# A two-layer hybrid mixer kernel: other start addresses of its buffers in SBUF, and another matmul cost in its planner

## The chip, the cores and the metric

The kernel runs on one core of one Trainium2 chip. The metric is the device time of one execution in microseconds (us), as the median of the runs shown. The core has five engines that run side by side: TensorE (PE, matrix multiplications; its weight loads are listed apart as PEld), VectorE (DVE), ScalarE (ACT), GpSimd (POOL) and SyncE (SP, which here only issues DMAs). Operands of the engines lie in SBUF, 128 partitions wide; a tile's address is its byte offset within each partition. Results of matmuls go to PSUM.

## What is computed

A sequence of 256 tokens of width 1024 goes through two layers in fp32. Each layer is a gated feed-forward block, a mixer with three branches (a gated linear recurrence, windowed attention, a gated delta rule), and another feed-forward block:

```
for l in range(2):
    x = x + 0.5 * swiglu(rms_norm(x, g1[l]), w_gate1[l], w_up1[l], w_down1[l])   # 1024 -> 2816 -> 1024
    u = rms_norm(x, gm[l])
    proj = u @ w_in[l]                                # 1024 -> 11536 columns
    ya, yb, yc = rg_lru(proj), attention(proj), delta_rule(proj)
    y = sum of sigmoid(gates) * (ya @ wa, yb @ wb, yc @ wc)
    x = x + y @ w_out[l]
    x = x + 0.5 * swiglu(rms_norm(x, g2[l]), w_gate2[l], w_up2[l], w_down2[l])
```

## The kernel before

**Tiling.** Activations are kept transposed, 128 channels on the partitions and the 256 tokens along the row: one such block is 128x256 fp32, 1024 bytes of each partition. Weights are read from HBM in blocks of up to 1024 columns into six buffers `raw0` to `raw5` (line 598 issues each DMA on SP's queue), and each block is split into two fp32r parts, `wh` (the rounded value, mostly by ACT) and `wl` (the rest, by DVE), in five buffers of each kind, 4096 bytes of a partition each. Activations are split in the same way. A product is then three fp32r matmuls that are added up in PSUM: high by high, low by high, high by low.

**The two forms of the main matmul.** In `stationary` (feed-forward and most of the mixer) a 128x128 piece of `wh` or `wl` is the stationary operand and a 256-column activation block is the moving one; a piece starts 512 bytes after the one before it. There are 11280 such matmuls. In `moving` (attention's queries, keys and values) the roles are swapped: 128 columns of an activation block are stationary, and 256 columns of `wh` or `wl` are moving. There are 864 of those. A first small product in each mixer uses pieces of only 64 columns. Beside these there are fp32 matmuls and transposes for the norms, the attention and the delta rule, whose operands lie mostly in one large tile, `arena`.

**Places in SBUF.** Tiles are placed one after the other, in the order in which `Prog.__init__` asks for them, each at a multiple of 32 bytes. `cst` begins at byte 16512. Before the change this gives `raw0` at 26560, `wh0` at 51136, `wl0` at 71616, `X` at 92096, then `zr`, `ssq`, `eps_n`, `half`, `tiny` at 102400, `arena` at 106496, and the 60 activation slots `s0` to `s59` (`Slots`, 1024 bytes each) from 163840. All sizes from `raw0` to `ssq` are multiples of 1024 bytes, and so are those of `tiny`, `arena` and the slots. So every `raw`, `wh`, `wl` buffer, `X`, `zr` and `ssq` begins 64 bytes below a multiple of 1024 (960 modulo 1024), and `tiny`, `arena` and all slots begin at one. Slots hold the split activations that the main matmuls read; a block of 256 columns that finds no slot free goes to `arena`, whose parts begin at multiples of 256 bytes.

**What sets the order.** The order of the instructions on each engine is fixed when the program is written out. `Prog` keeps a clock for each engine; each instruction that is written adds its estimated cost (`Engine._cost`) to its engine's clock. After every main matmul `pump` looks which side task (a conversion, a piece of the delta rule, a norm) is due by PE's clock, and writes its next step there. So PE's queue is one fixed sequence, the main matmuls with the side tasks' small matmuls between them, and the estimate for one main matmul decides after how many of them a side task's next step stands. The estimate for an fp32r matmul is

```
            if lhsT.dtype == F32R:
                return max(0.46 * n, 0.83 * m)
```

with n the moving and m the stationary columns: 0.46 x 256 = 117.8 ns.

Of the kernel before, what the change touches and what calls it, by code (L numbers as in the profile page):

```python
# [10 lines left out]
F32 = mybir.dt.float32  # L11
# [6 lines left out]
P = 128  # L18
# [21 lines left out]
KEEP, KEEP2 = 3072, 2048  # L40
ARENA_COLS = 14336
NSLOT = 60
SPARE = 4
SLACK = (800.0, 1500.0, 1500.0, 1500.0, 1500.0, 600.0)
URGENT = 2
# [54 lines left out]
def flat_chunks():  # L100
    return [c for layer in all_jobs() for jobs in layer for job in jobs for c in job[2]]


def group_chunks(chunks):
    groups, cur, cols = [], [], 0
    for c in chunks:
        w = c[3] * c[5]
        if cur and cols + w > GROUP_COLS:
            groups.append((cur, cols))
            cur, cols = [], 0  # L110
        cur.append(c)
        cols += w
    groups.append((cur, cols))
    return groups
# [60 lines left out]
class Arena:  # L175
    def __init__(self, pr, ap, unit):
        self.pr, self.ap, self.unit = pr, ap, unit
        self.n = ap.shape[1] // unit
        self.busy = [False] * self.n
        self.stamp = [0.0] * self.n  # L180
        self.peak = 0
# [123 lines left out]
def _free(ap):  # L305
    n = 1
    for x in ap.shape[1:]:
        n *= x
    return n


class Engine:
# [16 lines left out]
    def _cost(self, name, a, k):  # L329
        key = self._key  # L330
        if key == "pe":
            lhsT = k["lhsT"] if name == "matmul" else a[1]
            rhs = k["rhs"] if name == "matmul" else a[2]
            n, m = _free(rhs), _free(lhsT)
            if lhsT.dtype == F32R:
                return max(0.46 * n, 0.83 * m)
            if name == "transpose":
                return 0.84 * max(n, m)
            if m <= 32 and lhsT.shape[0] <= 32:
                return 40.0  # L340
            if m <= 64 and lhsT.shape[0] <= 64 and n <= 64:
                return 100.0
            return 1.7 * max(n, m)
        n = _free(a[0])
        if name == "tensor_reduce":
            n = _free(a[1])
        if key == "a":
            c = 93 + 0.833 * n
            for x in ("scale", "bias", "accum_out"):
                c += 93 * (not isinstance(k.get(x, 0.0), float) and x in k)  # L350
            func = a[2] if name == "activation" else None
            sets = TABLES.get(func)
            if sets and self._pr.table not in sets:
                self._pr.table = sets[0]
                c += 1283
            return c
        if key == "g":
            return (330 + 160 * n) if k.get("op") == ALU.pow else 350 + 0.6 * n
        if name == "reciprocal":
            return 68 + 6.3 * n  # L360
        fast = name in ("tensor_copy", "tensor_scalar") and a[1].space != PSUM
        c = 68 + (0.52 if fast else 1.04) * n
        if name in ("scalar_tensor_tensor", "tensor_scalar") and not isinstance(a[2], float):
            c += 60
        if k.get("accum_out") is not None:
            c += 60
        return c
# [5 lines left out]
class Prog:  # L373
    def __init__(self, ctx, tc, io):
        self.tc, self.nc, self.io = tc, tc.nc, io
        nc = self.nc
        self.clock = {"pe": 0.0, "v": 0.0, "a": 0.0, "g": 0.0}
        self.table = None
        self.cur = self.main = Task(None, 0.0, 0)
        self.step, self.used = set(), {}  # L380
        self.tasks = []
        self.pe, self.v = Engine(self, "pe", nc.tensor), Engine(self, "v", nc.vector)
        self.a, self.g = Engine(self, "a", nc.scalar), Engine(self, "g", nc.gpsimd)
        sb = ctx.enter_context(tc.tile_pool(name="sb", bufs=1))
        ps = ctx.enter_context(tc.tile_pool(name="ps", bufs=1, space=PSUM))
        dr = ctx.enter_context(tc.tile_pool(name="dr", bufs=1, space=bass.MemoryType.DRAM))
        self.cst = sb.tile([P, CST["_n"]], F32, name="cst")
        self.prm = sb.tile([P, L * PRM["_n"]], F32, name="prm")
        self.raw = [sb.tile([P, GROUP_COLS], F32, name=f"raw{i}") for i in range(NRAW)]
        self.wh = [sb.tile([P, 1024], F32R, name=f"wh{i}") for i in range(NCONV)]  # L390
        self.wl = [sb.tile([P, 1024], F32R, name=f"wl{i}") for i in range(NCONV)]
        self.X = sb.tile([P, KD, T], F32, name="X")
        self.zr = sb.tile([P, T], F32, name="zr")
        self.ssq = sb.tile([P, T], F32, name="ssq")
        self.eps_n = sb.tile([P, 1], F32, name="eps_n")
        self.half = sb.tile([P, 8], F32, name="half")
        self.tiny_t = sb.tile([P, 1024], F32, name="tiny")
        self.ar_t = sb.tile([P, ARENA_COLS], F32, name="arena")
        self.tiny = Arena(self, self.tiny_t, 8)
        self.slots = Slots(self, sb, NSLOT)  # L400
        self.ar = Arena(self, self.ar_t, 64)
        self.big = Banks(self, [ps.tile([P, 512], F32, name=f"big{i}") for i in range(NBIG)])
        self.sm = Banks(self, [ps.tile([P, 512], F32, name=f"sm{i}") for i in range(8 - NBIG)])
        self.gdram = [dr.tile([16, P], F32, name=f"gd{l}") for l in range(L)]
        self.rdram = [[dr.tile([P, 64], F32, name=f"rd{l}_{i}") for i in range(4)] for l in range(L)]
        self.rc = [self.tiny.get(16).ap for _ in range(L)]
        self.ea = [self.tiny.get(8) for _ in range(L)]
        self.qg = [self.tiny.get(6) for _ in range(L)]
        self.groups = group_chunks(flat_chunks())
        self.chunk_at = []  # L410
        off = 0
        self.goff = []
        for gi, (cs, cols) in enumerate(self.groups):
            self.goff.append(off)
            c0 = 0
            for c in cs:
                self.chunk_at.append((c, gi, c0, c[3] * c[5]))
                c0 += c[3] * c[5]
            off += P * cols
        self.unread = [len(cs) for cs, _ in self.groups]  # L420
        self.cursor = 0
        self.dma_next = 0
        self.dma_clock = 0.0
        self.raw_t = {}
        self.conv_t = {}
        self.conv_next = 0
        self.when = {}
        self.ops = {}
        self.prepared = set()
        self.nsq = None  # L430
        self.npair = 4
# [111 lines left out]
    def get(self, cols):  # L543
        b = None
        if cols == T:
            b = self.slots.get(F32, SPARE)
        return b or self.ar.get(cols, self.keep())
# [1157 lines left out]
```

## Time and profile before

| what | before |
|---|---|
| median of 3 runs | 1631.65 us (1627.21, 1631.65, 1632.0) |
| the profiled execution | 1627.63 us, of which the span from first to last instruction is 1625.4 us |
| granted TensorE clock, mean | 0.994 |
| PE busy | 1602.4 us (99%) |
| DVE, ACT, POOL busy | 71%, 58%, 9% |
| DMA | 279 MB, 172 GB/s, 54% of the 16 engines' time |

The stages in the profiled execution, by the first and last main matmul of each: layer 0 feed-forward 6 to 198 us, mixer 198 to 631, feed-forward 631 to 819; layer 1 feed-forward 819 to 1006, mixer 1006 to 1434, feed-forward 1434 to 1622. A record of a matmul is longer than the interval to the next one's start, since matmuls overlap in the array; the pace is read from starts. A row of the timeline merges instructions of one kind that follow each other, and one period of the main stream (three matmuls) takes two rows.

### The profile page before, as it was taken

To read this page: it belongs to the slowest core of one execution; us is meant where nothing else is said; L and a number is where in the kernel's file an instruction comes from. 1 tells how busy PE (TensorE), PEld (TensorE's weight loads), DVE (VectorE), ACT (ScalarE), POOL (GpSimd) and SP (SyncE) were. 2 spreads that over 40 slices of the span, in tenths; PEclk is the share of its full clock that TensorE was granted. 3 is DMA by queue.
4 is the path that set the end of the run, shared out by engine and by line. 5 is a ranking of instruction groups with operands and counts; after the bars stand their busy time and mean duration, and the time that the engine had idled before them with its cause. 6 is when DMAs were issued, how large, how long until landed. Compare 5 with 4: busy or idle time off the path is not lost. (4 is left out here: it accounts for less than half of the span.)

```text
span 1625.4 us, 34428 instructions
## 1 busy us (share of the span) xinstructions
PE 1602.4 (99%) x13952; PEld 1560.0 (96%) x13952; DVE 1159.2 (71%) x2172; ACT 936.7 (58%) x1643; POOL 139.3 (9%) x280
## 2 busy tenths in 40 slices
PE   9999999999999999999999999999999999999999
PEld 8999999989988999999999999999898899999999
DVE  8666588987973667666566656989878756676653
ACT  7544456878854546444454445568887555554442
POOL 0000000345002000000000000003540120000000
PEclk9999999999998999999999999999999999999999
DMA  8655656544343565555555555656443345655562
GB/s 304 186 187 179 193 179 194 164 162 133 120 129 107 163 204 184 187 188 178 188 192 183 182 185 185 195 176 182 139 140 122 123 131 189 190 184 185 181 188 86
DMA packets 84942, 279.04 MB, mean 172 GB/s; under 512 B 10256, under 2 KB 15664, under 8 KB 84784
## 3 DMA queue, kind: packets, MB, share of 16 engines
q1 hardware_dynamic: 84784, 276.85, 53.7%
q8 instruction: 109, 1.79, 0.4%
q14 instruction: 49, 0.40, 0.1%
HBM read 275.49 MB, written 1.33 MB: 170 GB/s over the span
## 5 line engine op out<-in xcount | busy, mean ns | idle before, releaser
L323 PE MATMUL big<-s,wh 128*128 128x256 f32 (+1 forms) x7520 | 1346.3, 281 | 7.0 <-DVE s L323 6.0
L323 PEld LDWEIGHTS big<-s,wh 128*128 128x128 f32 (+1 forms) x7520 | 1151.0, 188 | 17.4 <-DVE s L323 6.8
L323 PE MATMUL big<-s,wl 128*128 128x256 f32 (+1 forms) x3760 | 1053.6, 280 | 0.0
L323 DVE TENSOR_TENSOR wl<-raw,wh 128x1024 fp32r<-128x1024 f32 (+3 forms) x523 | 620.8, 1187 | 248.4 <-ACT wh L323 245.2
L323 ACT ACTIVATE wh<-raw 128x1024 fp32r<-128x1024 f32 (+4 forms) x497 | 509.1, 1025 | 361.8 <-PE big L323 168.8
L323 PEld LDWEIGHTS big<-s,wl 128*128 128x128 f32 (+1 forms) x3760 | 705.3, 188 | 2.8 <-issue 1.8
L323 ACT ACTIVATE s<-s 128x256 fp32r<-128x256 f32 (+1 forms) x213 | 85.2, 413 | 116.6 <-DVE s L323 116.0
L323 POOL TENSOR_TENSOR tiny<-tiny,half 128x4 f32<-128x4 f32 (+1 forms) x28 | 38.6, 1378 | 1102.0 <-DVE tiny L323 1083.9
L323 PE MATMUL sm<-arena 128*128 128x128 f32 (+7 forms) x1440 | 114.0, 238 | 9.7 <-DVE arena L323 6.9
L323 PEld LDWEIGHTS sm<-arena 32*32 32x32 f32 (+5 forms) x1440 | 85.8, 138 | 30.2 <-issue 9.3
L323 PE MATMUL big<-wh,s 128*128 128x256 f32 x576 | 110.2, 287 | 0.0
L323 POOL TENSOR_TENSOR arena<-arena 128x60 f32<-128x60 f32 (+14 forms) x240 | 98.6, 411 | 62.6 <-DMA arena<-rd 44.7
L323 DVE TENSOR_TENSOR s<-s,s 128x256 fp32r<-128x256 f32 (+1 forms) x181 | 75.7, 422 | 36.5 <-ACT s L323 36.1
L323 PEld LDWEIGHTS big<-wh,s 128*128 128x128 f32 x576 | 89.6, 189 | 1.2
L323 DVE SCALAR_TENSOR_TENSOR s<-big,prm,s 128x255 f32<-128x255 f32 (+2 forms) x183 | 85.6, 477 | 6.6 <-ACT s L323 5.3
L323 DVE TENSOR_TENSOR arena<-big,zr 128x512 f32<-128x512 f32 x88 | 60.9, 692 | 34.8 <-PE big L323 34.5
L323 PE MATMUL big<-wl,s 128*128 128x256 f32 x288 | 82.1, 285 | 0.0
L323 ACT ACT_TABLE_LOAD x63 | 80.8, 1283 | 1.7 <-PEq L1697 0.7
L323 ACT ACTIVATE arena<-sm 128x128 f32<-128x128 f32 (+6 forms) x152 | 48.8, 323 | 37.6 <-PE sm L323 35.1
L323 ACT ACTIVATE s<-big 128x256 f32<-128x256 f32 x53 | 20.2, 382 | 62.1 <-PE big L323 62.1
L323 PEld LDWEIGHTS big<-wl,s 128*128 128x128 f32 x288 | 54.5, 189 | 0.4
L323 ACT ACTIVATE s<-big,prm 128x256 f32<-128x256 f32 x53 | 26.5, 499 | 45.2 <-PE big L323 45.0
(110 smaller groups left out, 772.3 us busy)
## 6 DMA issues: line engine op xcount, KB each, us to landing
raw<-wts SPq DMA_DIRECT2D x435, 512.0 KB, 3.7
raw<-wts SPq DMA_DIRECT2D x64, 448.0 KB, 3.6
raw<-wts SPq DMA_DIRECT2D x16, 384.0 KB, 3.1
arena<-rd SPq DMA_DIRECT2D x8, 512.0 KB
arena<-rgw SPq DMA_DIRECT2D x4, 512.0 KB, 5.2
arena<-gd SPq DMA_DIRECT2D x16, 128.0 KB, 4.7
X<-x SPq DMA_DIRECT2D x4, 256.0 KB, 4.9
raw<-wts SPq DMA_DIRECT2D x4, 256.0 KB, 3.2
```

The costliest lines, as they stand in the source:

```text
L323: r = f(*a, **k)
```

## The change

`eps_n` and `half` are placed ahead of the weight buffers; a tile of 252 floats that nothing uses follows them; and one of 32 floats that nothing uses stands between `arena` and the slots. With each start at a multiple of 32 bytes, `raw0` then begins at byte 27648 = 27 x 1024. `raw`, `wh`, `wl`, `X`, `zr`, `ssq`, `tiny` and `arena` all begin at multiples of 1024, and the slots 128 bytes past such multiples. The planner's estimate for an fp32r matmul becomes 0.445 x 256 = 113.9 ns. No instruction is added or taken away.

```diff
+PAD = 252
+SHIFT = 32
@@
             if lhsT.dtype == F32R:
-                return max(0.46 * n, 0.83 * m)
+                return max(0.445 * n, 0.83 * m)
@@
         self.prm = sb.tile([P, L * PRM["_n"]], F32, name="prm")
+        self.eps_n = sb.tile([P, 1], F32, name="eps_n")
+        self.half = sb.tile([P, 8], F32, name="half")
+        sb.tile([P, PAD], F32, name="pad")
         self.raw = [sb.tile([P, GROUP_COLS], F32, name=f"raw{i}") for i in range(NRAW)]
@@
         self.ssq = sb.tile([P, T], F32, name="ssq")
-        self.eps_n = sb.tile([P, 1], F32, name="eps_n")
-        self.half = sb.tile([P, 8], F32, name="half")
         self.tiny_t = sb.tile([P, 1024], F32, name="tiny")
         self.ar_t = sb.tile([P, ARENA_COLS], F32, name="arena")
+        sb.tile([P, SHIFT], F32, name="shift")
```

## Rows read from the trace of the kernel before

**Rows 1.** The page: busy time of each engine; granted clock in 40 slices.
```profile
PE 1602.4 (99%) x13952; PEld 1560.0 (96%) x13952; DVE 1159.2 (71%) x2172; ACT 936.7 (58%) x1643; POOL 139.3 (9%) x280
...
PEclk9999999999998999999999999999999999999999
```

**Rows 2.** Groups by form, PE: line, operation, shapes, count | busy, mean ns | idle before.
```profile
L323 PE MATMUL big<-s,wh 128*128 128x256 f32 x7488 | 1340.4, 281 | 6.6 <-DVE s L323 5.6 <-ACT s L323 0.3 <-ACT wh L323 0.2
L323 PE MATMUL big<-s,wl 128*128 128x256 f32 x3744 | 1049.2, 280 | 0.0
L323 PE MATMUL big<-wh,s 128*128 128x256 f32 x576 | 110.2, 287 | 0.0
L323 PE MATMUL big<-wl,s 128*128 128x256 f32 x288 | 82.1, 285 | 0.0
```

**Rows 3.** Stretches: length, busy time (count) of PE, PEld, DVE, ACT, POOL, clock, DMA.
```profile
20.00:196.00 176.00, 176.00 (x1497) 176.00 (x1496) 119.10 (x184) 89.87 (x128) 0.00 (x0) 1.00 0.62 197
...
539.30:633.70 94.40, 94.21 (x831) 94.01 (x831) 66.08 (x97) 50.59 (x76) 0.00 (x0) 1.00 0.61 198
...
641.00:817.00 176.00, 176.00 (x1496) 176.00 (x1496) 115.05 (x150) 85.00 (x122) 0.00 (x0) 1.00 0.58 186
```

**Rows 4.** Timeline of PE near 700 us: start, length, operation, count.
```profile
699.84 0.40 PE L323 MATMUL big<-s,wh 128*128 128x256 f32 x2
...
701.96 0.28 PE L323 MATMUL big<-s,wh 128*128 128x256 f32 x1
```

**Rows 5.** The same near 600 us.
```profile
599.78 0.39 PE L323 MATMUL big<-s,wh 128*128 128x256 f32 x2
...
601.82 0.39 PE L323 MATMUL big<-s,wh 128*128 128x256 f32 x2
```

**Rows 6.** Timeline of PE where the faster stretch begins, and where it ends.
```profile
539.95 0.60 PE L323 MATMUL sm<-cst,arena 128*128 128x128 f32 x4
...
540.51 0.28 PE L323 MATMUL big<-s,wl 128*128 128x256 f32 x1
...
540.85 0.28 PE L323 MATMUL big<-s,wl 128*128 128x256 f32 x1
...
634.99 0.59 PE L323 MATMUL sm<-ssq,cst 128*128 128x256 f32 x2
```

**Rows 7.** Timeline of PE in the swapped form, near 394 to 400 us.
```profile
394.98 0.28 PE L323 MATMUL big<-wl,s 128*128 128x256 f32 x1
...
400.08 0.28 PE L323 MATMUL big<-wl,s 128*128 128x256 f32 x1
```

**Rows 8.** The same form near 358 us.
```profile
358.11 0.28 PE L323 MATMUL big<-wl,s 128*128 128x256 f32 x1
...
358.81 0.28 PE L323 MATMUL big<-wl,s 128*128 128x256 f32 x1
```

**Rows 9.** Timeline of PE: fp32 transposes, one after the other.
```profile
413.12 0.27 PE L323 MATMUL sm<-cst,arena 128*128 128x128 f32 x1
...
413.88 0.27 PE L323 MATMUL sm<-cst,s 128*128 128x128 f32 x1
```

**Rows 10.** Stretches inside the mixers, columns as in rows 3.
```profile
340.00:440.00 100.00, 95.40 (x944) 88.94 (x944) 83.99 (x225) 81.47 (x200) 39.99 (x72) 0.98 0.38 121
...
510.50:524.10 13.60, 11.35 (x118) 9.21 (x118) 4.94 (x12) 5.65 (x16) 0.00 (x0) 0.50 0.07 25
...
1140.00:1240.00 100.00, 94.27 (x966) 87.69 (x965) 84.94 (x232) 83.66 (x205) 40.84 (x72) 1.00 0.42 128
```

**Rows 11.** Groups by form, DVE: the same shape with operands in different tiles.
```profile
L323 DVE TENSOR_TENSOR s<-s,s 128x256 f32<-128x256 f32 x62 | 25.8, 421 | 0.4
...
L323 DVE TENSOR_TENSOR ssq<-ssq,s 128x256 f32<-128x256 f32 x39 | 16.3, 418 | 0.2
...
L323 DVE TENSOR_TENSOR arena<-arena,s 128x256 f32<-128x256 f32 x18 | 7.6, 425 | 0.6
```

**Rows 12.** DMA issues: count, KB each, median us from issue to landing.
```profile
raw<-wts SPq DMA_DIRECT2D x435, 512.0 KB, 3.7
```

**Rows 13.** Waits: engine and tile that waited, for whom: us, times, longest.
```profile
PE sm L323 <- DVE arena L323: 8.6, 8, 2.2
PE big L323 <- DVE s L323: 6.0, 10, 2.3
```

## The prediction

> **What bounds the kernel now.** I read the page first: PE is busy for 1602.4 of 1625.4 us, and its clock is full except for a short stretch [rows 1]. The waits of PE for other engines are small: the two largest are 8.6 and 6.0 us [rows 13]. So the time is the number of PE's instructions times their pace, and the question is what the pace is. The groups by form give the numbers: 7488 + 3744 main matmuls with a weight piece stationary (and 48 more with 64 columns, 11280 together) and 576 + 288 in the swapped form [rows 2]. Their mean length (281 ns) is no pace, because they overlap; starts are. In the second feed-forward of layer 0 six periods of three matmuls lie between 699.84 and 701.96 us [rows 4]: 2.12 us / 18 = 117.8 ns. The stretch around it says the same over 176 us: 1496 records, of which about two were already running at its edge, so 176 / 1494 = 117.8 ns, and so does the first feed-forward with 1497 [rows 3].
>
> The view that matters most comes next: the same form, same clock, same addresses, but near 600 us. There six periods take 601.82 - 599.78 = 2.04 us, or 113.3 ns each matmul [rows 5]. This faster pace begins right behind four small fp32 operations at 539.95 us (540.85 - 540.51 = 0.34 us a period) and is gone after the two of the norm at 634.99 us [rows 6]; between them the stream ran 831 matmuls in 94.4 us [rows 3]. DVE and ACT are as busy there as elsewhere in feed-forward (70% and 54% against 68% and 51% at 20 to 196 us), and the DMA share is 0.61 against 0.62, so it is not their load that decides. A stream of main matmuls therefore has at least two steady paces, 117.8 and 113.3 ns; which one it takes is settled at its start, by how weight loads and moving reads lie against each other in time, and it keeps it until something breaks the stream.
>
> The swapped form has both too: 394.98 to 400.08 us is 15 periods in 5.10 us, 113.3 ns [rows 7], while 358.11 to 358.81 us is two in 0.70 us, 116.7 ns [rows 8]. With weights at 960 modulo 1024 and slots at 0, the stationary operand starts 64 bytes before the moving one (modulo 512) in the usual form, and 64 bytes after it in the swapped one. The usual form is at the faster pace in one long stretch only, about 830 of 11280; the swapped form often. So the relative start address is a plausible cause of which pace a stream settles on: it shifts the two reads against each other as a shift in time would.
>
> **The change, part by part.**
>
> *The addresses.* After it the two operands start 128 bytes apart (modulo 256) in both forms. No row shows that distance. From below the cost per matmul is bounded by the fastest back-to-back instructions of similar length in the trace, transposes with seven intervals in 413.88 - 413.12 = 0.76 us, 108.6 ns [rows 9]; from above, by no more than one further step of the same size, 117.8 + 4.5 = 122.3 ns, an estimate. I take the nearer of the observed two that isn't the present one, 113.3 ns: it is a pace that this very stream holds for 94 us at a time, so it needs no state that the trace doesn't have, and the distance moves away from the one at which the slower pace is taken nearly always. The step is 117.8 - 113.3 = 4.5 ns.
>
> How many gain it: 11280 less the 830 that have it already, 10450, times 4.5 ns = 47.0 us. Of the swapped form I take 0.4 of 864 as slow (an estimate, between the two kinds of stretch): 346 x 4.5 = 1.6 us. Gross 48.6 us, of which the two mixers hold about 4900 matmuls, 22 us, and feed-forward the rest.
>
> In feed-forward nothing eats the gain: PE has no gap in 176 us, DVE is busy 68%, and the DMA share is 0.62 with 3.7 us from issue to landing [rows 3, 12]; 4% more pace makes these 71% and 0.64. In the mixers part of it is lost. From 340 to 440 us and 1140 to 1240 us PE is busy 94 to 95%, DVE 84 to 85%, ACT 81 to 84% [rows 10]; steps of the delta rule there wait on DVE, ACT and a DMA round trip, and these don't get shorter. From 510.5 to 524.1 us in layer 0 PE has only such steps left and stands at half clock (0.50, the lower of the two levels, 1.2 GHz) [rows 10]. Of the 1910 records in the two dense stretches some 1600 (an estimate) are main matmuls and would gain 7 us; I take half of that as turned into waits, 3.5 us, and 2.5 us more because layer 0's last pair is waited for anyway: together 6 us, with 0 and 13 (all of the dense stretches, and 6 for the tail) as ends. What is late next there is PE's wait for DVE's `arena` results, now 8.6 us [rows 13].
>
> *DVE, ACT, DMA at other addresses.* DVE's 128x256 operation costs 421 ns with all operands in slots, 418 with `ssq` (960 modulo 1024) beside a slot, and 425 with `arena` beside one [rows 11]. Their distances differ and the cost doesn't, so I price it at nothing; if 7 ns (425 - 418) fell on each of some 1000 such operations it would be 7 us of an engine that is idle 29% of the time, hidden by PE's stream. The transfers into `raw` begin elsewhere but are the same in number and size; at 62% they have room. The unused tiles cost no instruction.
>
> *The planner.* Each main matmul counts 113.9 ns instead of 117.8, so a side task's step stands behind 3.4% more of them. If the pace falls to 113.3 ns the plan fits the chip as it did before (117.8 planned and measured), and the order change is worth little: from -3 to +4 us, by what one stall like that at 510 to 524 us may gain or lose (13.6 us, in part at half clock) [rows 10]. I take nothing.
>
> *The sum.* Against the profiled execution: 1627.6 - 48.6 + 6 = 1585 us. The median of the runs is 4 us above that execution; the fast stretch at 539 to 634 us is worth 830 x 4.5 = 3.7 us, so it is likely that the slower two runs lacked such a stretch. With the fast pace everywhere the difference vanishes; I leave 2 us for streams that still start slow: 1587 us.
>
> **A rule that speaks against it.** The trace shows two paces at one set of addresses [rows 4, 5]. The Trainium skill, "TensorE: Matmul & The Clock Gate", section "Part 2: What happens when you issue a matmul", says that moving and stationary operands have read ports of their own, so that loading the next weights takes no SBUF bandwidth from the running matmul. By that rule addresses are indifferent and the time stays; it is rival 2 below. The trace agrees with it in part at most: the two paces show that something besides the column count sets the interval, though not that it is an SBUF conflict.
>
> **The rivals.** 1, *streams settle at either pace*: the new distance only shifts the odds, as in the swapped form. At half and half the gain is 24 us and 3 are lost: 1631.7 - 21 = 1611 us. For it: the swapped form mixes within microseconds. Against: the fast stretch at 539 us holds for 94 us.
> 2, *the change doesn't do what it says*: addresses don't matter, and only the phase after a break does. The pace stays at 117.8, and the planner is off by 3.4%, which costs up to 4 us or gains 3: 1631 us (1627 to 1636). For it: one address has both paces. Against: the same clock and load in both forms, yet different shares.
> 3, *slower*: the new distance lets the two reads meet more often, and each stream settles a step higher. It decides as soon as more than some 1000 matmuls (5 us) take 122.3 ns; all 11280 would cost 50.8 us, less 3 that waits absorb: 1679 us. For it: nothing shows 128 bytes to be far from a conflict. Against: no long stretch of that pace is in the trace.
> 4, *faster still*: the pace falls to the 108.6 ns of the transposes, 9.2 ns less: 10450 x 9.2 + 830 x 4.7 + 864 x 6.5 = 106 us, less some 15 lost in the mixers: 1537 us. No long stretch shows it.
>
> **How the numbers follow.** Forecast 0.62 (its own range 1577 to 1603: 13 us lost instead of 6, or streams of one stage slow), rival 1 0.10, rival 2 0.14, rival 3 0.09, rival 4 0.05. The likeliest gives 1587 us. From 1577 to 1633 us lie the forecast, rival 1 and most of rival 2, 0.84 in all; that is the range. A measurement of this kernel can tell about 0.3%, 5 us. Faster by more than that: forecast, rivals 1 and 4, and a little of rival 2, 0.78; within it: most of rival 2, 0.12; slower: rival 3 and the rest of rival 2, 0.10.
>
> **What would show it.** Right: in the trace after, 18 main matmuls in 2.04 us in both feed-forwards of both layers, with the counts of instructions unchanged; DVE's 128x256 operations still at 418 to 425 ns; and PE's idle time up by some 6 us, in the mixers alone. Wrong: periods of 0.353 us as now (rival 2), 0.367 (rival 3) or 0.326 (rival 4) in feed-forward, or a stall in a mixer of more than 13 us that eats the gain.

## The result, and the profile after

| what | before | after |
|---|---|---|
| median of 15 runs each, side by side | 1631.24 us (1623.0 to 1632.89) | 1638.66 us (1634.45 to 1641.56) |
| the profiled execution | 1627.63 us, span 1625.4 us | 1639.39 us, span 1637.3 us |
| granted TensorE clock, mean | 0.994 | 0.998 |

The change makes the kernel slower: after / before is 1.0057, with a 95% interval of 1.0045 to 1.0068, some 9 us of 1631. The prediction said 1587 us, 1577 to 1633.

The page of after, busy time of each engine and the granted clock in 40 slices, answers to [rows 1]:

```profile
PE 1617.2 (99%) x13952; PEld 1574.8 (96%) x13952; DVE 1151.3 (70%) x2157; ACT 939.2 (57%) x1657; POOL 141.9 (9%) x280
...
PEclk9999999999999999999999999999999999999999
```

PE has the same 13952 instructions as before and is busy 14.8 us longer (DVE has 15 fewer and ACT 14 more, as in planner_alone below, so the planner's estimate moves a few steps between engines); the span grew by 11.9 us, so PE's idle time even shrank by 2.9 us. The clock is, if anything, a little better. The groups by form (line, operation, shapes, count | busy, mean ns | idle before) show the same counts as [rows 2] with longer records, 284, 283, 291 and 289 ns where 281, 280, 287 and 285 stood:

```profile
L325 PE MATMUL big<-s,wh 128*128 128x256 f32 x7488 | 1360.9, 284 | 7.8 <-DVE s L325 4.4 <-ACT wh L325 1.2 <-ACT s L325 1.0
...
L325 PE MATMUL big<-s,wl 128*128 128x256 f32 x3744 | 1060.4, 283 | 0.1
...
L325 PE MATMUL big<-wh,s 128*128 128x256 f32 x576 | 112.8, 291 | 0.0
...
L325 PE MATMUL big<-wl,s 128*128 128x256 f32 x288 | 83.2, 289 | 0.0
```

The pace itself stands in the stretches of after (columns as in rows 3), two of which answer to [rows 3]:

```profile
20.00:196.00 176.00, 176.00 (x1486) 176.00 (x1485) 117.48 (x185) 90.77 (x128) 0.00 (x0) 1.00 0.60 195
641.00:817.00 176.00, 176.00 (x1469) 176.00 (x1469) 111.69 (x148) 84.04 (x121) 0.00 (x0) 1.00 0.57 183
```

In the same 176 us, PE never idle and at full clock in both kernels, there are 1486 and 1469 matmuls where there were 1497 and 1496. Less the two that already run at a stretch's edge, these are 176 / 1484 = 118.6 and 176 / 1467 = 120.0 ns, against 117.8. The timeline of PE near 700 us (start, length, operation, count) shows the second of these in every period, as [rows 4] did for 117.8 ns:

```profile
699.75 0.40 PE L325 MATMUL big<-s,wh 128*128 128x256 f32 x2
...
702.27 0.41 PE L325 MATMUL big<-s,wh 128*128 128x256 f32 x2
```

Seven periods of three lie between these two rows: 2.52 us / 21 = 120.0 ns. Nothing like [rows 5], 113.3 ns at the end of layer 0's mixer, is left: no dozen matmuls in a row of after, in any stage, average below 116.6 ns. Single intervals tell more. In the second feed-forward, at 120.0 ns, they alternate between 121 and 119 ns. In the other three they go round in a cycle of about 115, 117, 122, 120 and 119 ns; the mean of single intervals is 118.7 ns there, which the count of records in a stretch gives as 118.6.

The mixers changed in two directions. These are the stretches of after that answer to [rows 10]:

```profile
340.00:440.00 100.00, 97.38 (x1052) 90.57 (x1052) 83.60 (x222) 86.01 (x205) 39.41 (x71) 1.00 0.41 126
510.50:524.10 13.60, 13.60 (x203) 12.59 (x202) 7.77 (x14) 6.07 (x13) 0.00 (x0) 1.00 0.41 126
1140.00:1240.00 100.00, 94.13 (x1012) 87.35 (x1011) 77.14 (x215) 76.02 (x184) 49.31 (x90) 0.98 0.42 130
```

The gap at 510 to 524 us, where PE stood at clock 0.50 with 118 instructions, is gone: 203 instructions, no idle time, clock 1.00. PE has main matmuls left for that stretch now. Measured from its first to its last main matmul, layer 0's mixer went from 433.2 to 429.7 us, and layer 1's from 428.0 to 436.0. The four feed-forwards went from 191.9, 187.3, 187.3 and 187.3 us to 193.0, 190.7, 188.7 and 188.7. That is 7.3 us more in the feed-forwards and 4.5 in the mixers, 11.8 together: the whole growth of the span.

### The profile page after: what moved, and what is told of

It reads as the page before. It is cut to its first block, busy times and chain, and to the rows that moved or that the text cites. A ratio compares the mean times of both kernels' runs of the same rounds, so it can differ in the third digit from the quotient of the medians.

```text
span 1637.3 us, 34442 instructions
## 1 busy us (share of the span) xinstructions
PE 1617.2 (99%) x13952; PEld 1574.8 (96%) x13952; DVE 1151.3 (70%) x2157; ACT 939.2 (57%) x1657; POOL 141.9 (9%) x280
## 5 line engine op out<-in xcount | busy, mean ns | idle before, releaser
L325 PE MATMUL big<-s,wh 128*128 128x256 f32 (+1 forms) x7520 | 1366.9, 284 | 8.1 <-DVE s L325 4.7
L325 PE MATMUL big<-s,wl 128*128 128x256 f32 (+1 forms) x3760 | 1064.8, 283 | 0.1
L325 ACT ACTIVATE wh<-raw 128x1024 fp32r<-128x1024 f32 (+3 forms) x496 | 509.2, 1027 | 472.8 <-issue 258.6
L325 POOL TENSOR_TENSOR tiny<-tiny,half 128x4 f32<-128x4 f32 (+1 forms) x28 | 42.9, 1535 | 1092.6 <-DVE tiny L325 1044.0
L325 PE MATMUL sm<-arena 16*32 16x16 f32 (+8 forms) x1424 | 109.3, 233 | 5.8 <-DVE tiny L325 4.8
L325 PEld LDWEIGHTS sm<-arena 32*32 32x32 f32 (+5 forms) x1424 | 81.8, 134 | 24.3 <-issue 9.2
L325 POOL TENSOR_TENSOR arena<-arena 128x60 f32<-128x60 f32 (+14 forms) x240 | 94.5, 394 | 91.1 <-DMA arena<-rd 51.9
L325 DVE SCALAR_TENSOR_TENSOR s<-big,prm,s 128x255 f32<-128x255 f32 (+2 forms) x174 | 81.9, 476 | 13.8 <-ACT s L325 12.4
```

What stands on the lines that cost most here:

```text
L325: r = f(*a, **k)
```

## The experiments

Two theories stood at the start. One is that the addresses set the pace. The other is that the addresses are indifferent, and that the planner's new estimate costs the time through another order of the side tasks. If it was the addresses, it was open whether the distance between the two operands decides or the places themselves.

### Each half of the change alone

planner_alone is the kernel before with the new estimate; addresses_alone is the kernel after with the old one.

```diff
planner_alone (from before):
-                return max(0.46 * n, 0.83 * m)
+                return max(0.445 * n, 0.83 * m)
addresses_alone (from after):
-                return max(0.445 * n, 0.83 * m)
+                return max(0.46 * n, 0.83 * m)
```

> The kernel before with the planner's estimate at 0.445 per moving column and nothing else changed: addresses as before. Theory 1 (the new addresses made the main stream slower; the new order is worth little): the pace stays at 117.8 ns with a chance of stretches at 113.3, and the time lies within 4 us of the kernel before, 1627 to 1635 us. Theory 2 (the new order costs it: side steps stand further back and more waits end late): slower than before by most of the 7 us that the change cost, 1636 to 1640 us, at an unchanged pace.

> The addresses of the changed kernel with the planner's estimate at 0.46 as before. Theory 1: the main matmuls repeat the intervals of the changed kernel (115 to 122 ns, mean 118.7 to 120.0 instead of 117.8), 12144 x 0.9 to 1.4 ns = 11 to 17 us more, of which waits in the mixers take back some: 1637 to 1647 us. Theory 2: as the kernel before, 1627 to 1635 us.

Measured beside the same runs of before (median 1627.88 us): planner_alone 1625.85 us, 0.999 with an interval of 0.9973 to 1.0008; addresses_alone 1641.16 us, 1.0087 with 1.0057 to 1.0117. PE's stretches (length, PE busy (count), clock, DMA share, GB/s) of planner_alone,

```profile
20.00:196.00 176.00, 176.00 (x1497) 1.00 0.59 196
...
840.00:980.00 140.00, 140.00 (x1191) 1.00 0.55 182
```

and of addresses_alone:

```profile
20.00:196.00 176.00, 176.00 (x1469) 1.00 0.59 193
641.00:817.00 176.00, 175.87 (x1481) 1.00 0.55 183
840.00:980.00 140.00, 140.00 (x1182) 1.00 0.54 182
```

The planner's estimate leaves the pace at 117.8 ns (176 / 1495); the addresses alone bring 120.0 (176 / 1467) in the first feed-forward and 118.6 (140 / 1180) in the third. The stretch from 641 us on holds the break that the norm's small matmuls make near a stage's start, so its count tells less. So the addresses are the cause of the loss. The planner is the cause of the new order: the stretch at 510 to 524 us of planner_alone, with the addresses of before, is full as well, and that of addresses_alone is not (columns as in rows 10):

```profile
510.50:524.10 13.60, 13.60 (x206) 12.52 (x205) 6.37 (x12) 7.04 (x18) 0.00 (x0) 1.00 0.44 147
...
510.50:524.10 13.60, 9.99 (x141) 7.47 (x139) 6.96 (x15) 5.56 (x15) 2.40 (x9) 0.64 0.22 69
```

With the new order layer 0's mixer is 5.5 us shorter (433.2 to 427.7) and layer 1's 5.6 longer (428.0 to 433.6): nothing in sum. These are single executions, though, and the 433.2 us of before hold the fast stretch of [rows 6], 830 x 4.5 = 3.7 us, which planner_alone lacks.

### The same distance at other places, and a bare stream

distance_64 puts the slots 64 bytes past multiples of 1024 and the weights at multiples: the distance of before at other absolute places.

```diff
-SHIFT = 32
+SHIFT = 16
-                return max(0.445 * n, 0.83 * m)
+                return max(0.46 * n, 0.83 * m)
```

> Weight buffers at multiples of 1024 bytes as in the changed kernel, the activation slots 64 bytes past such multiples: the distance of the kernel before at other absolute addresses; planner at 0.46. If only the distance of the two operands counts, the intervals of the main matmuls are those of before: 117.8 ns, now and then 113.3. If absolute places count, they differ from 117.8, and the alternating 119 and 121 of the changed kernel may stay.

It ran in 1629.56 us (one run), with 1496 and 1497 matmuls in the two stretches of 176 us: 117.8 ns, the pace of before. Another absolute place with the same distance gave the same pace.

```profile
20.00:196.00 176.00, 176.00 (x1496) 1.00 0.60 196
641.00:817.00 176.00, 176.00 (x1497) 1.00 0.55 186
```

probe_distance, like all kernels here whose name begins with probe, leaves the model out. It is a bare stream of the main matmul in the kernel's order (high by high, high by low, low by high, pieces 512 bytes apart, blocks 1024 bytes apart). Each distance (start of the moving operand less that of the stationary one) gets three streams of 168 matmuls (120 to 168 in the later probes), one behind each of three beginnings: two fp32 matmuls of 128 columns, one of 256, eight small ones of 32.

```diff
+DISTANCES = [32 * i for i in range(16)]
...
+        for d in DISTANCES:
+            for k in range(BREAKS):
...
+                c = d // 4
+                for t in range(TRIPLES):
...
+                    xh = slice(c + (n % 4) * T, c + (n % 4) * T + T)
+                    xl = slice(c + 1024 + (n % 4) * T, c + 1024 + (n % 4) * T + T)
+                    nc.tensor.matmul(out, lhsT=w[:, ws], rhs=s[:, xh], start=first, stop=False)
+                    nc.tensor.matmul(out, lhsT=w[:, ws], rhs=s[:, xl], start=False, stop=False)
+                    nc.tensor.matmul(out, lhsT=w[:, wl], rhs=s[:, xh], start=False, stop=last)
```

> Not the model: a bare stream of fp32r matmuls in the pattern of the main stream (triples of 128x128 pieces 512 bytes apart, 256 moving columns), no other engine at work. Sixteen distances between moving and stationary start, 0 to 480 bytes in steps of 32, three streams of 168 matmuls each, each begun behind another kind of fp32 matmul. If the distance sets the pace, each distance has its own intervals: 117.8 or 113.3 ns at 64, a mix with 119 to 122 ns at 128, and some distance is faster than both. If the phase in which a stream starts sets it, the three streams of one distance differ. If neither counts without other engines at work, all run at one pace, 113.3 ns or below.

The stretches (columns as in rows 3) for distances 0, 32, 64 and 128, and for 192 behind each of the three beginnings:

```profile
12.00:28.00 16.00, 16.00 (x136) 16.00 (x135) 0.00 (x0) 0.00 (x0) 0.00 (x0) 1.00 0.00 1
75.00:91.00 16.00, 16.00 (x139) 16.00 (x139) 0.00 (x0) 0.00 (x0) 0.00 (x0) 1.00 0.00 1
136.00:152.00 16.00, 16.00 (x138) 16.00 (x138) 0.00 (x0) 0.00 (x0) 0.00 (x0) 1.00 0.00 1
259.00:275.00 16.00, 16.00 (x137) 16.00 (x136) 0.00 (x0) 0.00 (x0) 0.00 (x0) 1.00 0.00 1
381.00:396.00 15.00, 15.00 (x135) 15.00 (x134) 0.00 (x0) 0.00 (x0) 0.00 (x0) 1.00 0.00 1
401.00:417.00 16.00, 16.00 (x138) 16.00 (x137) 0.00 (x0) 0.00 (x0) 0.00 (x0) 1.00 0.00 1
422.00:437.00 15.00, 15.00 (x135) 15.00 (x134) 0.00 (x0) 0.00 (x0) 0.00 (x0) 1.00 0.00 1
```

DVE, ACT and POOL have no instruction there and the DMA share is 0.00, yet the counts differ from distance to distance at full clock. The mean interval between starts, over each stream but its first dozen matmuls, is 120.0 ns at 0, 116.7 at 32, 117.8 at 64, 120.0 at 96, 118.7 at 128 and 160, 113.3 or 117.8 at 192 and 118.3 at 224; from 256 on the row repeats. So PE alone makes the pace, out of where its two operands lie. At 64 it is the pace of before, at 128 that of three of after's four feed-forwards, and 113.3 ns is to be had at 192. The 120.0 ns of after's second feed-forward did not come up at 128.

### Three more distances in the whole kernel

Three of these distances were then tried in the kernel with the old estimate.

```diff
distance_192:
-SHIFT = 32
+SHIFT = 48
distance_32:
-SHIFT = 32
+SHIFT = 8
distance_0:
-        sb.tile([P, SHIFT], F32, name="shift")
```

> Weight buffers at multiples of 1024 bytes, slots 192 bytes past such multiples, planner at 0.46. Theory 1 (the pace is a function of the distance modulo 256 bytes, and at 192 of the way in which the stream began): feed-forward in long stretches of 113.3 or 117.8 ns, the swapped form (distance 64) all at 117.8. If half the matmuls are at 113.3, 11280 x 0.5 x 4.45 = 25 us less, with 2 more in the swapped form and some 5 lost to waits: about 1610 us; 1580 if nearly all, 1632 if hardly any. Theory 2 (the full model's other engines set the pace, the probe doesn't carry over): 117.8 or 118.7 ns, 1627 to 1645 us.

> Slots 32 bytes past multiples of 1024, weights at such multiples, planner at 0.46. Theory 1: main matmuls at 116.7 ns, the swapped form (distance 224) at 118.3: 11280 x 1.1 = 12 us less, 2 more: 1617 to 1622 us, a little faster than before and without luck in how a stream begins. Theory 2: 1627 to 1645 us.

> Weight buffers, arena and slots all at multiples of 1024 bytes, planner at 0.46. Theory 1: all main matmuls at 120.0 ns without alternation: 11280 x 2.2 = 25 us and 864 x 4 = 3.5 us more than before, less a few that waits take back: 1650 to 1660 us. Theory 2: as the kernel before or the changed one, 1627 to 1645 us.

| distance | bare stream | kernel, feed-forwards | time beside before at 1628.81 us | ratio, 95% interval |
|---|---|---|---|---|
| 0 | 120.0 ns | 120.0 ns | 1654.52 us | 1.0149 (1.0127 to 1.0171) |
| 32 | 116.7 (one stream of probe_fine 117.8) | 116.7 | 1619.29 us | 0.9939 (0.9916 to 0.9962) |
| 192 | 113.3 or 117.8 | 113.3 or 117.8 | 1612.13 us | 0.9876 (0.9842 to 0.991) |

PE's stretches of distance_192 show both of its paces in one execution: 170 / 1501 = 113.3 ns in the first feed-forward, and 140 / 1189 = 117.7 in the third. Long parts of both its mixers run at 113.3 ns too. The third feed-forwards of distance_32 and distance_0 follow (140 / 1200 = 116.7 and 140 / 1167 = 120.0).

```profile
20.00:190.00 170.00, 170.00 (x1503) 1.00 0.63 203
840.00:980.00 140.00, 140.00 (x1191) 1.00 0.56 183
...
840.00:980.00 140.00, 140.00 (x1202) 1.00 0.56 186
...
840.00:980.00 140.00, 140.00 (x1169) 1.00 0.55 179
```

Its times spread over 17 us, 1599.83 to 1616.56, more than those of any kernel with one pace. That each execution takes the faster pace in other stages would explain it; only one execution has a trace, so this is argued and not shown. distance_192 is faster than before and than after.

### Finer steps, and a pace that didn't carry over

probe_fine repeats the bare stream for distances in steps of 8 bytes, probe_word for 4, 12, ..., 252.

```diff
probe_fine:
-DISTANCES = [32 * i for i in range(16)]
+DISTANCES = [8 * i for i in range(32)]
probe_word:
-DISTANCES = [32 * i for i in range(16)]
+DISTANCES = [4 + 8 * i for i in range(32)]
```

> The bare stream again, 32 distances from 0 to 248 bytes in steps of 8, three streams of 120 matmuls each, begun behind two fp32 matmuls of 128 columns, one of 256, and eight of 32. The multiples of 32 repeat the first probe's paces (120.0, 116.7, 117.8, 120.0, 118.7, 118.7, 113.3 or 117.8, 118.3 ns). If the distance acts in steps of a word, the distances between are as different from each other; if in lines of 16 or 32 bytes, they equal their neighbours. A distance that gives 113.3 ns behind all three beginnings would be the better place for the slots.

> The bare stream at the 32 distances that the second probe left out, 4 to 252 bytes in steps of 8. If lines of 16 bytes count, each equals a neighbour that is a multiple of 8, and 116 or 108 gives 113.3 like 112; if words count, the landscape goes on without order and some distance may be below 113.3 ns, down to the 108.6 of the fp32 transposes.

The paces have no order that one could follow: 118.3 ns at 48, 117.8 at 64, 121.1 at 72, 120.0 at 104, 113.3 at 112 behind all three beginnings, 121 to 122 at 120, 118.7 at 128, 120 to 122 at 136. The odd words lie between 116.7 and 123.4 ns; 108 and 116 give 120.0 and 121.7, not the 113.3 of their neighbour 112, so single words count. Nothing lies below 113.3.

112 looked best, since its fast pace needs no luck at the beginning. Slots begin at multiples of 32, so for distance_112 and distance_112_planned the weights were moved to 16 bytes past such a multiple instead, the second with the new estimate; `wl` is moved in the same way as `wh`.

```diff
-        self.wh = [sb.tile([P, 1024], F32R, name=f"wh{i}") for i in range(NCONV)]
+        wh = sb.tile([P, NCONV * 1024 + 256], F32R, name="wh")
+        self.wh = [wh[:, 4 + i * 1024:4 + (i + 1) * 1024] for i in range(NCONV)]
```

> Weight parts in one tile for the high and one for the low halves, each part 16 bytes past a multiple of 1024, slots 128 bytes past: distance 112, which no multiple of 32 gives. Planner at 0.46. Theory 1 (the distance modulo 256 sets the pace): 113.3 ns in all stages behind any beginning, 11280 x 4.4 = 50 us less than before, 2.4 more in the swapped form (distance 144: 118.7 ns), some 5 lost to waits in the mixers: 1583 to 1592 us. Theory 2 (the bare stream's 113.3 at 112 is not kept when other engines work, or after other beginnings): a mix with 117 to 122 ns, 1605 to 1640 us.

> The same places with the planner's estimate at 0.445, 113.9 ns, which then is close to the pace. Theory 1: the pace as at 0.46, the time within 5 us of it, since the order was worth little at the old pace; a gain of more than 5 us would say that a fitting plan matters once the pace has fallen.

Both are slower than before (1629.05 us): 1650.71 us, 1.0132 (1.0117 to 1.0147), and 1647.54 us, 1.0122 (1.0105 to 1.0139). distance_112 lies above the ranges of both of its theories. The new estimate is worth some 3 us here, with intervals that overlap. PE's stretches of distance_112 in the second and third feed-forward are at 120.0 ns (140 / 1167 in the third; the other stretch holds the break by the norm near the stage's start):

```profile
641.00:817.00 176.00, 175.90 (x1464) 1.00 0.57 181
840.00:980.00 140.00, 140.00 (x1169) 1.00 0.57 180
```

So the theory that the distance alone sets the pace fell.

### What else counts: the places, and the weight's columns

probe_absolute sets the weights 0, 16, 32, 48, 64 and 128 bytes past a multiple of 1024, each with three distances. probe_columns keeps the moving reads and narrows the stationary operand from 128 to 64 and 32 columns.

```diff
probe_absolute:
+DISTANCES = [(a, d) for d in (112, 64, 192) for a in (0, 16, 32, 48, 64, 128)]
probe_columns:
+DISTANCES = [(d, m) for d in (0, 64, 112, 128, 192) for m in (128, 64, 32)]
```

> The bare stream at distances 112, 64 and 192 with the weights themselves 0, 16, 32, 48, 64 and 128 bytes past a multiple of 1024, three beginnings each. If only the distance counts, the paces at one distance are equal for all six; distance 112 with the weights at 16 is then 113.3 ns as at 0, and what undid it in the full kernel was something else that runs there. If the place of the weights counts too, 112 at 16 shows the 116.7 to 120.0 ns of the full kernel, and places 32 or 64 apart agree.

> The bare stream with stationary pieces of 128, 64 and 32 columns (the moving ones stay at 256), at distances 0, 64, 112, 128 and 192, three beginnings each. If the two reads get in each other's way, the part of the interval above some 109 ns goes down with the columns of the weight read: at distance 0 from 120 ns to about 114 at 64 columns and 111 at 32, and the differences between distances shrink alike. If the moving read alone sets the interval, by where it starts, the columns change nothing.

At distance 112 the weights at 0, 32, 64 and 128 give 113.3 ns, those at 16 and 48 give 120.0, each behind all three beginnings. PE's stretches for the weights at 0 and at 16:

```profile
47.00:60.00 13.00, 13.00 (x117) 1.00 0.01 1
81.00:94.00 13.00, 13.00 (x111) 1.00 0.00 1
```

So the place modulo 32 counts beside the distance, and the 120.0 ns of two of distance_112's feed-forwards is what its places give in the bare stream too, here and in probe_places (the other two, at 118.4 and 116.7 ns, have paces that it didn't show). distance_64 could not show this: it moved the weights by 64 bytes, a multiple of 32.

probe_absolute also says more of the distance of before. At distance 64, with the weights at 64 or 128, the streams behind the first two beginnings ran at 117.8 ns and those behind the third at 113.3; with them at 0 or 32 all ran at 117.8. Here are the first and the third beginning with the weights at 64:

```profile
531.00:544.00 13.00, 13.00 (x113) 1.00 0.00 1
567.00:580.00 13.00, 13.00 (x117) 1.00 0.00 1
```

So the two paces of before at one pair of places [rows 4, 5] have a likeness in a stream with PE alone at work.

The stationary operand matters in its own right. With the moving operand 128 bytes past a multiple of 1024, weights at 0 give 118.7 ns (probe_distance), at 16 give 120.0, and at 64 give 117.8 or 113.3 (probe_absolute), so it is not the place of the moving operand alone. With moving reads at the same places, 128 columns at distance 128 give 118.7 ns and 64 columns 116.7, at distance 0 120.0 against 113.3 behind two of the beginnings, but at distance 192 113.3 or 117.8 against 119.05. PE's stretches at distance 0, with 128 and with 64 columns:

```profile
55.00:70.00 15.00, 15.00 (x128) 1.00 0.00 1
95.00:110.00 15.00, 15.00 (x135) 1.00 0.01 2
```

With 32 columns most streams ran at 113.3 ns and none below, though 117.8, 116.7 and 120.0 came up too. A smaller weight load changes the pace, but not always for the better, so the expected fall in step with the columns did not come. That the two rows of reads mesh well or badly in time would fit this; no run shows it.

### What picks among several paces

At 192 two paces are possible. distance_192_split asks whether the fp32 matmul before a stream picks one: the norm's sum becomes two matmuls of 128 columns in place of one of 256, as in the beginnings of the bare stream.

```diff
-        self.pe.matmul(ps[:, :T], lhsT=self.c("ones"), rhs=self.ssq, start=True, stop=True)
+        for c in range(0, T, P):
+            self.pe.matmul(ps[:, c:c + P], lhsT=self.c("ones"), rhs=self.ssq[:, c:c + P], start=True, stop=True)
```

> Distance 192 as before, and the fp32 matmul of the norms, which falls into the main stream a few matmuls after each stage's start, is issued as two of 128 columns instead of one of 256. Theory 1 (at 192 two paces exist, and the small work that breaks a stream picks which): behind two of 128 columns the probe's streams ran at 113.3, behind one of 256 at 117.8 ns; so the feed-forwards of layer 0 (second) and layer 1 (both), at 117.8 in the run with distance 192, fall to 113.3: 3 x 1579 x 4.45 = 21 us less than that run's 1612, 1587 to 1596 us. Theory 2 (the choice is by chance, or set by other engines): 1605 to 1616 us.

1614.27 us, 0.9914 (0.9887 to 0.994). The faster pace moved from the first feed-forward to the last one (130 / 1148 = 113.2 ns), and the first now has 117.8:

```profile
20.00:196.00 176.00, 176.00 (x1496) 1.00 0.59 196
...
1470.00:1600.00 130.00, 130.00 (x1150) 1.00 0.55 173
```

The size of that matmul doesn't pick the pace. The bare streams agree: with the weights at 0 and distance 192, the stream behind two matmuls of 128 columns ran at 113.3 ns in probe_distance and at 117.8 in probe_absolute, and the one behind a matmul of 256 columns the other way round. These are the two of probe_absolute, in that order, to set beside the two of probe_distance at 381 and 401 us above:

```profile
636.00:649.00 13.00, 13.00 (x113) 1.00 0.00 1
653.00:666.00 13.00, 13.00 (x118) 1.00 0.00 1
```

So neither the places nor the matmuls just ahead of a stream fix which of its paces it takes; what does, stays open.

probe_places and place_24_192 looked for a pair of places with the fast pace in both forms. The bare stream had weights 8, 16 and 24 bytes past a multiple of 1024 and the moving operand at multiples of 32; the kernel has the weights at 24 and the slots at 192 (`wl` alike).

```diff
probe_places:
+DISTANCES = [(a, (s - a) % 256) for a in (8, 16, 24) for s in range(0, 256, 32)]
place_24_192 (from distance_192):
+        self.wh = [wh[:, 6 + i * 1024:6 + (i + 1) * 1024] for i in range(NCONV)]
```

> The bare stream with weights 8, 16 or 24 bytes past a multiple of 1024 and the moving operand at each multiple of 32 within 256 bytes. With the weights at 16 and the moving operand at 128 (the places of the run with distance 112) it shows 116.7 to 120.0 ns if the place counts, 113.3 if only the distance does. By the first reading no place has to be faster than 113.3 ns; if some combination has 113.3 behind all three beginnings, it is a place that the slots can have.

> Each weight part 24 bytes past a multiple of 1024 and the slots 192 past, planner at 0.46. In the bare stream these places gave 113.3, 116.7 and 113.3 ns behind the three beginnings. Theory 1 (the pace is a function of both places and of the beginning, and what the bare stream shows for the pair of places is kept by the full kernel): only these two paces in feed-forward; at a half of each, 11280 x (117.7 - 115.0) = 30 us less, about 4 more in the swapped form (weights moving 88 bytes behind the slots: 120 ns by the first probes), 4 lost to waits: 1600 to 1610 us; about 1590 if 113.3 prevails, 1617 if 116.7 does. Theory 2 (the bare stream's paces are kept by the full kernel only where the weights stand at multiples of 32): anything from 117 to 122 ns, 1625 us or more.

In the bare stream 24 and 192 gave 113.3, 116.7 and 113.3 ns; the others lie between 115.5 and 120.1 but for two streams at 121.9 and 123.4. The kernel took 1612.9 us, 0.9883 (0.9854 to 0.9913), no better than distance_192. Its feed-forwards ran at 116.7 ns in layer 0 and 120.0 in layer 1, as the second and third show, and long parts of its mixers at 113.3:

```profile
650.00:790.00 140.00, 140.00 (x1203) 1.00 0.59 185
840.00:980.00 140.00, 140.00 (x1169) 1.00 0.57 180
```

120.0 is none of the bare stream's three. A bare stream shows which paces are near, but three beginnings don't show all that one pair of places has.

## Why the prediction was wrong

*What bounds the kernel: right.* PE is busy 99% in both kernels, and 11.8 us of stage times against 11.9 us of span leave nothing else to explain. Waits of PE were not it. After's largest, which answer to [rows 13], are smaller than those of before:

```profile
PE sm L325 <- DVE tiny L325: 4.8, 3, 2.3
PE big L325 <- DVE s L325: 4.7, 9, 1.6
PE sm L325 <- DVE arena L325: 1.7, 3, 0.7
```

*That relative addresses set the pace: right in kind.* addresses_alone and the bare stream show it, so rival 2 fell. The reading of [rows 4] and [rows 5] was right as well: one pair of places can have more than one steady pace (113.3 or 117.8 at 192, 118.7 or 120.0 in after). The stretch near 600 us lies in layer 0's mixer, though, while the prediction sets it beside DVE and ACT "elsewhere in feed-forward" as if it were one. That the pace is settled "by how weight loads and moving reads lie against each other in time" is not shown: in the trace of before a weight load's record starts 2 to 4 ns after a matmul's both near 600 and near 700 us, and what settles it stayed open above.

*The pace at the new distance: the step that failed.* "I take the nearer of the observed two that isn't the present one, 113.3 ns", and "the distance moves away from the one at which the slower pace is taken nearly always". The runs showed 118.7 ns in three feed-forwards and 120.0 in one (0.356 and 0.360 us a period, between the signs named for rivals 2 and 3). That lies inside the bounds set, 108.6 and 122.3, but on the other side of 117.8. Two things were wrong in it. It took an order for granted, in which one moves away from a bad distance towards better ones, and probe_fine shows none. And it took a pace seen at one distance as evidence for another. What the trace did contain was two distances, 64 in the usual form and -64, which is 192, in the swapped one. The first was slow nearly always, the second often fast [rows 7]; the bare stream is alike, mostly at 117.8 ns at 64 and mostly at 113.3 at 192. The trace spoke for 192, the distance with which the kernel does get faster, and said nothing of 128. With no row for the new distance the honest range ran from one bound to the other, and the chance of slower was no less than that of faster.

*The terms.* 10450 + 346 matmuls were to gain 4.5 ns each, 48.6 us. In place of that, the 6336 main matmuls of the feed-forwards lost 7.3 us, 1.15 ns each. In the mixers the mean of uninterrupted intervals (under 160 ns) rose from 116.99 to 118.72 ns in the usual form and from 115.42 to 118.78 in the swapped one: 4944 x 1.73 + 864 x 3.36 = 8.6 + 2.9 = 11.5 us, of which 4.5 show. For addresses_alone nearly the same sum, 11.6 us, stands against 8.8 us in the mixers (861.2 to 870.0). So the new order gave after some 4 us back beside the new addresses. Beside the old ones it shows nothing in sum, but there 3.7 us of fast stretch in before may hide a gain of that size. The intervals of the two ratios, 1.0045 to 1.0068 and 1.0057 to 1.0117, overlap, so this 4 us is not settled. The prediction's own split was off as well: of its 48.6 us the mixers' share is not 22 us, since the 830 that already were fast lie there, but (4944 - 830) x 4.5 + 1.6 = 20 us. The 6 us that waits were to take back had no gain to work on.

*Rival 3 had the sign, and its size was off.* It said that the two reads meet more often and each stream settles a step higher. The second half came true; that reads meet is not shown. It priced the step at 4.5 ns and 51 us; it was 0.9 to 2.2 ns in the feed-forwards, and 9 us by the ratio. With a chance of 0.09 and no part in the range, it was treated as if only a full step could happen, although it was said to decide from 5 us on.

*The rule weighed against the change.* By the Trainium skill, "TensorE: Matmul & The Clock Gate", section "Part 2: What happens when you issue a matmul", the two operands have read ports of their own and loading weights takes no SBUF read bandwidth from a running matmul. In probe_distance, with no other engine at work, the same instructions took 120.0 ns at distance 0 and 113.3 at 192, and in probe_columns a narrower weight load changed the pace of the same moving reads. The measurement decides: in these fp32r streams the pace hangs on both operands together, so rival 2, drawn from that page, is out. Whether they meet at SBUF's ports or elsewhere no run shows.

*DVE at other addresses: right, nothing.* The groups of after that answer to [rows 11] have 418, 418 and 426 ns where 421, 418 and 425 stood:

```profile
L325 DVE TENSOR_TENSOR s<-s,s 128x256 f32<-128x256 f32 x64 | 26.2, 418 | 0.3
...
L325 DVE TENSOR_TENSOR ssq<-ssq,s 128x256 f32<-128x256 f32 x39 | 16.3, 418 | 0.2
...
L325 DVE TENSOR_TENSOR arena<-arena,s 128x256 f32<-128x256 f32 x16 | 6.8, 426 | 0.5
```

*The planner: right, from -3 to +4 us and taken as nothing.* planner_alone is 0.999 of before, -4.4 to +1.3 us by its interval. The mechanism named for it, the gap at 510 to 524 us, did close; in the same trace the other mixer is 5.6 us longer.

*The 4 us between the profiled execution and the median of before* were put down to the fast stretch of [rows 6]. No run here has two traces of one kernel, so this stays open.

## What to carry to other kernels

When PE is busy 99% at full clock, its time is a count times a pace, and the pace of a stream of weight loads and matmuls depends on where both operands start in SBUF, here from 113.3 to 120.0 ns in whole feed-forwards where before had 117.8 (4% less to 2% more). No rule for good places came out of these runs, so don't reason from one pair of places to another: time a bare stream at the places in question, behind several beginnings, and then the kernel, which can still settle on a pace that the bare stream didn't show. When a number for the new case is in no row, let the range reach both bounds and keep both signs open.

## What the runs showed of the hardware that was not expected

- One fp32r matmul of 256 columns with its own 128-column weight load takes 113.3 to 123.4 ns in a steady stream, with nothing but PE at work. In steps of 32 bytes with the weights at a multiple of 1024, the pace repeats with the distance modulo 256; at distance 112 it changed between weights at multiples of 32 (113.3) and 16 past them (120.0).
- A stream repeats a short cycle of unequal intervals, such as 121 and 119 ns, or 115, 117, 122, 120 and 119, and one pair of places can have several such cycles. What makes them, and what picks one, was not found.
- 113.3 ns was the floor in every stream tried, and 192 bytes between weights and slots gave it in part of the kernel: SHIFT = 48 with the old estimate is 0.9876 of before. Distance 112 with the weights at multiples of 32, where the bare stream had nothing else, was not tried in the kernel: tiles begin at multiples of 32. Slots cut out of one wider tile, as the weights were for distance_112, would have allowed it, so the most promising place stands untested.
